# Even and odd token tiles as the two halves, block sums during the attention, and the first feed-forward products in two column parts

## The chip, the cores and the metric

The kernel runs on one core of a Trainium2 chip. The metric is the device time of one execution in microseconds. TensorE (PE) multiplies matrices, VectorE (DVE), ScalarE (ACT) and GpSimd (POOL) do the elementwise work, and SyncE (SP) issues most of the transfers. Each engine works through its own queue in order.

## The reference

Two encoder layers work on 1024 tokens of 1024 channels. In each, a norm and one input projection feed three mixers: a Fourier mix over all tokens, attention in a window (eight query heads, two key groups, blocks of 128 tokens, a learned sink), and attention to 256 memory rows. The three results are normalised apart and go through one output projection. Then comes a gated feed-forward of 2816 channels.

```python
y = jnp.concatenate([_rmsnorm(y_f, ...), _rmsnorm(y_a, ...), _rmsnorm(y_m, ...)], axis=-1) @ w_out[l]
x = x + _rmsnorm(y, g_post_mix[l])
h = _rmsnorm(x, g_pre_ffn[l])
gate, up = jnp.split(h @ w_ffn_in[l], 2, axis=-1)
f = (jax.nn.silu(gate) * up) @ w_ffn_out[l]
x = x + _rmsnorm(f, g_post_ffn[l])
```

## The kernel before

**Arithmetic.** Each operand is split into a high and a low part: ACT casts the high one (line 151), DVE or POOL subtracts it from the source (line 152). One product of two operands is three products on PE: high by high, high by low, low by high. The two feed-forward products are made by Strassen's scheme. The input h is cut into four blocks of 512 channels by 512 tokens (two halves of the channels, two halves of the tokens), and seven products are made of sums of them. `Blocks.tile` turns one token tile of 128 into the four raw blocks: eight transposes `hTp` (line 1033) and two ACT copies (line 1034). `Blocks.sum(i, c)` makes the operand of product i for the columns of one tile (chunk c of four): a sum where the product needs one (line 1051, on POOL for i = 6, else on DVE) and its split. `Blocks.last` (lines 1063 and 1064) makes the differences for products 7 and 3 in place. Weights come in pairs of 128 output columns (`Quad`), a gate quad and an up quad for each of 11 pairs. `weights(i)` makes a sum of weight blocks (line 1094, DVE) and its split, and `product` issues 12 products of 512 columns (line 1104). Products 2 and 4 share the PSUM tile `qy`, 5 and 3 `qz`, 1 and 7 `qx`, and 6 has `qw`.

**Token halves.** Half 0 is tiles 0 to 3, half 1 is tiles 4 to 7, in all stages. Products 2 and 4 need half 0 alone; 5, 1, 6, 7 and 3 need half 1 too.

**The stage around the change.** The window attention runs twice over the eight tiles, once for each key group. The first pass is woven with the other two mixers' output product (`fm_units`). In the second pass, `out_prep(t)` splits both groups' results of tile t (POOL makes the low parts), squares them on ACT, sums the squares with four small products `ssp` (line 925) and takes the root on POOL (line 929). `out(t)` makes the output product `mo` of tile t (24 products), scales it (line 1008, DVE), and goes through the residual norm: square on ACT (line 322), root on POOL (lines 208 and 210), multiply (line 324, DVE), add (line 325, POOL, for the last tile DVE), then the norm ahead of the feed-forward: square (284), root, multiply (289, DVE). After that the tile can be transposed. The loop has eight tiles and a tail of four steps in which the block sums are written; the sums for products 2 and 4 come at steps 8 and 9, the others from step 8 on.

**The order.** The code gives the work in this sequence, and a scheduler with its own costs places each instruction in its engine's queue. Buffers are slots of two arenas by number (`Ring`, `at`), so what may be written when follows from those numbers. The attention's keys, queries and output weights lie in slots that block operands take over later: product 6's operand (slots 32 and 40) lies where the output weights are until the last `mo`.

## Time and profile before

| | |
|---|---|
| median of three runs | 2135.3 us (2132.69 to 2136.14) |
| profiled execution | 2135.5 us, span 2133.7 us |
| mean granted TensorE clock | 0.969 |
| busy: PE, DVE, ACT, POOL | 2013.2, 1577.7, 1060.6, 863.4 us |
| PE busy, 400 to 420 us | 7.29 of 20 us |
| PE busy, 440 to 460 us | 20.00 of 20 us |

A profile row names the line, the engine, what is written and read, the shape and the count. A row of the timeline begins with its start and its duration; a bracket gives the idle time ahead of it and what ended it. A row of the windows gives the stretch and its length, then the busy time of PE, of its weight loads, of DVE, ACT and POOL with the number of instructions, then the granted clock, the share of the transfer engines and GB/s. Rows of the chain of waits give start, duration and what ran. Layer 0 has the way into the feed-forward at about 400 us, layer 1 at about 1450 us.

### The profile page before, as it was taken

What the parts mean: (1) busy time and instruction counts of PE and PEld (TensorE: products, weight loads), DVE (VectorE), ACT (ScalarE), POOL (GpSimd) and SP (SyncE); (2) the same over time, 40 slices, a digit from 0 to 9 for tenths busy, and PEclk for the clock granted to TensorE, in tenths of its full rate; (3) what the DMA queues carried; (4) which work ended last, traced back from release to release, by engine and by line L of the source; (5) the groups of instructions that cost most, each with busy time, mean ns of one, the idle gap of its engine ahead of it and who ended that gap; (6) DMA issues with size and microseconds to landing.
All of it is one profiled execution on the core that took longest, in us unless ns stands there. A gap on an engine that the chain in (4) does not pass through costs nothing.

```text
span 2133.7 us, 28334 instructions
## 1 busy us (share of the span) xinstructions
PE 2013.2 (94%) x9490; PEld 1655.0 (78%) x9490; DVE 1577.7 (74%) x2441; ACT 1060.6 (50%) x2257; POOL 863.4 (40%) x858
## 2 busy tenths in 40 slices
...
GB/s 221 45 50 65 65 94 105 152 65 94 118 101 95 112 94 194 318 221 287 246 138 41 60 64 85 75 137 110 84 129 94 94 111 92 123 249 284 276 261 138
DMA packets 173602, 287.50 MB, mean 135 GB/s; under 512 B 15480, under 2 KB 73360, under 8 KB 173456
## 3 DMA queue, kind: packets, MB, share of 16 engines
...
q8 instruction: 74, 1.21, 0.2%
...
## 4 chain that ended last, share of the span: by engine, by line
PE 74%; DMA 8%; DVE 7%; ACT 4%; POOL 4%; issue 2%; SPq 0%; POOLq 0%; DVEq 0%; ACTq 0%
PE fo L1232 12%; PE qz L1104 11%; PE qx L1104 11%; PE qy L1104 11%; PE mo L162 7%; PE qw L1104 5%; PE kvp L162 4%; PE qp L162 3%; DVE arena_r L152 3%; DMA arena_f<-actd 2%; PE sc L728 2%; PE pT L765 2%; DMA arena_f<-in_w_ffn_out 1%; ACT arena_r L151 1%; PE zT L162 1%
## 5 line engine op out<-in xcount | busy, mean ns | idle before, releaser
L151 ACT CAST arena_r<-arena_f 128x512 fp32r<-128x512 f32 (+1 forms) x780 | 443.1, 591 | 674.0 <-PE qz L1104 115.5
L152 DVE TENSOR_TENSOR arena_r<-arena_f,arena_r 128x512 fp32r<-128x512 f32 (+1 forms) x676 | 536.6, 816 | 182.9 <-ACT arena_r L151 179.6
L1232 PE MATMUL fo<-arena_r 128*128 128x512 f32 x1848 | 432.2, 395 | 17.5 <-ACT arena_r L151 15.1
L1232 PEld LDWEIGHTS fo<-arena_r 128*128 128x128 f32 x1848 | 351.7, 191 | 94.6 <-ACT arena_r L151 17.7
L1104 PE MATMUL qy<-arena_r 128*128 128x512 f32 x1056 | 261.5, 397 | 27.6 <-ACT arena_r L151 16.5
L1104 PEld LDWEIGHTS qy<-arena_r 128*128 128x128 f32 x1056 | 201.5, 192 | 72.0 <-ACT arena_r L151 17.0
L1094 DVE TENSOR_TENSOR arena_f<-arena_f 128x512 f32<-128x512 f32 x220 | 206.0, 939 | 5.1
L1104 PE MATMUL qz<-arena_r 128*128 128x512 f32 x704 | 196.3, 389 | 1.8 <-DVE arena_r L152 1.8
L1124 POOL TENSOR_TENSOR arena_f<-arena_f 128x512 f32<-128x512 f32 x44 | 73.0, 1658 | 292.8 <-ACT arena_f L1109 292.8
L1216 POOL TENSOR_TENSOR arena_f<-arena_f 128x512 f32<-128x512 f32 x50 | 73.6, 1475 | 269.5 <-DVE arena_r L152 136.2
L1104 PEld LDWEIGHTS qz<-arena_r 128*128 128x128 f32 x704 | 132.0, 188 | 29.8 <-DVE arena_r L152 2.4
L1156 POOL TENSOR_TENSOR arena_f<-arena_f 128x512 f32<-128x512 f32 x44 | 73.6, 1674 | 165.6 <-DVE arena_f L1136 119.1
L152 POOL TENSOR_TENSOR arena_r<-arena_f,arena_r 128x256 fp32r<-128x256 f32 (+2 forms) x104 | 88.8, 859 | 118.4 <-ACT arena_r L151 93.3
L1104 PE MATMUL qx<-arena_r 128*128 128x512 f32 x528 | 127.7, 389 | 1.4 <-ACT arena_r L151 1.4
L1104 PE MATMUL qw<-arena_r 128*128 128x512 f32 x528 | 127.6, 389 | 0.0
L1104 PE MATMUL qx<-big,arena_r 128*128 128x512 f32 x528 | 126.8, 389 | 0.0
L1104 PEld LDWEIGHTS qx<-arena_r 128*128 128x128 f32 x528 | 99.1, 188 | 22.5 <-ACT arena_r L151 2.0
L1104 PE MATMUL qz<-big,arena_r 128*128 128x512 f32 x352 | 115.5, 389 | 0.0
L1104 PEld LDWEIGHTS qw<-arena_r 128*128 128x128 f32 x528 | 99.1, 188 | 20.8
L1104 PEld LDWEIGHTS qx<-big,arena_r 128*128 128x128 f32 x528 | 99.1, 188 | 20.6
L162 PE MATMUL mo<-arena_r 128*128 128x512 f32 x384 | 102.6, 406 | 5.5 <-POOL arena_r L152 4.0
L162 PE MATMUL mo<-big,arena_r 128*128 128x512 f32 x384 | 102.3, 404 | 0.0
...
## 6 DMA issues: line engine op xcount, KB each, us to landing
...
actd<-arena_f SPq DMA_DIRECT2D x154, 256.0 KB, 3.7
arena_f<-actd SPq DMA_DIRECT2D x154, 256.0 KB, 4.2
...
```

The source lines that it names most:

```text
L151: nc.scalar.copy(hi, src)
L152: return (lo_eng or nc.vector).tensor_tensor(out=lo, in0=src, in1=f32(hi), op=ALU.subtract)
L162: mm(self.dst, a, b, start=self.i == 0, stop=self.i == self.n - 1)
L728: mm(pt, lhs, self.kst[g][i][:, k0 * P : k1 * P], start=i == 0, stop=i == 1)
L765: nc.tensor.transpose(pT[:, h, :], es_[h // 2][:, h % 2, j * P : j * P + P], ident)
L1094: nc.vector.tensor_tensor(out=s, in0=a, in1=b, op=op)
L1104: mm(pt, a, b, start=start and n == 0, stop=n == 11, skip_group_check=not start)
L1124: nc.gpsimd.tensor_tensor(out=self.v, in0=self.v, in1=self.s2, op=ALU.add)
L1156: (G if i in (0, 3) else V).tensor_tensor(out=a[i], in0=c, in1=g[i], op=ALU.mult)
L1216: (nc.vector, nc.gpsimd)[k % 2].tensor_tensor(out=s, in0=x, in1=y, op=op)
L1232: mm(pt, ab[:, 0, x, sl], ab[:, 1, y], start=new and first and j == 0, stop=last and j == 2, skip_group_check=not new)
```

## The change

Five things are changed. Even tiles are now half 0 and odd tiles half 1, so `divmod(t, 4)` becomes `divmod(t, 2)` with the roles exchanged, and the stages that go through tiles by halves take them in the order 0, 2, 4, 6, 1, 3, 5, 7. The attention keeps the order 0 to 7. A chunk of 128 columns then has all its four raw blocks after two neighbouring tiles.

The loop makes sums of chunks 0 to 2 from step 4 on rather than in the tail. Only chunk 3 needs the last two tiles.

The first group's half of `out_prep` (split, squares, two of four `ssp` products) is made in the first pass by `ya_prep`, and the second pass adds its sum of squares to the stored one.

Products 2 and 4 of the first gate and up quads are made in two column parts, 384 columns as soon as chunks 0 to 2 are there and 128 later (`ahead`). The weight operand is made once and used by both parts.

Buffers move: block operands, weights, raw weights and the sums' slot; the operands of the second feed-forward product have nine slots rather than six in layer 0 (`abs_`, seven for its last product), and the same fifteen in another order in layer 1.

The diff, cut to what is spoken of. Left out are renamed indices, the Fourier stage's sums over tiles (the same six additions), and the tile order in the start and in the last stage:

```diff
@@ -38,7 +38,9 @@
...
 SKEW = 1
-N_SM = {"pos": 1}
+
+TILES = (0, 2, 4, 6, 1, 3, 5, 7)
+N_SM = {"pos": 1, "ssa": 2}
 PS_BUFS = {"sc": 2, "pT": 2, "av": 2, "pd": 2}
...
@@ -125,15 +127,15 @@
...
     ropes = {2: run(6, 4, 0.5), 8: run(36, 6, 2)}
-    ems, es_ring, y1s = run(16, 4, 2), run(33, 5, 3), run(6, 2, 1)
+    ems, es_ring, y0s, y1s = run(16, 4, 2), run(33, 5, 3), run(8, 2, 1), run(6, 2, 1)
     sqs, pms, xfs = run(16, 2, 2), run(20, 2, 2), Ring(16, 20, 24, 28, 32, 0)
-    qws, sns, silus, acts = Ring(32, 0, 16, 20), Ring(36, 38, 40, 42, 32, 34), run(8, 5, 2), run(18, 7, 2)
-    sums, wsums = run(8, 4, 2), Ring(4, 6)
+    qws, sns, silus, acts = Ring(8, 12, 0, 44), Ring(36, 38, 40, 42, 32, 34), run(8, 5, 2), run(18, 7, 2)
+    sums, wsums = Ring(14), Ring(4, 6)
     ras, rbs, bsums, xs_ = run(40, 3, 2), run(46, 6, 2), Ring(58, 32, 34), Ring(36, 24)
...
     zzs, dhs, tabs = run(112, 2, 4), run(64, 2, 4), run(72, 4, 2)
-    mps, phs, yys = run(24, 2, 4), run(16, 3, 4), run(104, 2, 4)
-    wcs, abs_ = Ring(112, 116, 96, 100, 48, 52, 56, 60), Ring(80)
+    mps, phs, yys, y1y = run(24, 2, 4), run(16, 3, 4), run(104, 2, 4), run(104, 4, 2)
+    wcs, abs_ = Ring(24, 28, 112, 116, 120, 48, 52, 56), Ring(80)
...
@@ -291,7 +293,7 @@
...
-        half, c = divmod(t, 4)
+        c, half = divmod(t, 2)
         if c == 0:
...
@@ -789,8 +793,7 @@
...
                 nc.gpsimd.tensor_tensor(out=self.v32[:, 4 * half : 4 * half + 4], in0=f32(v[:, :, 0]), in1=f32(v[:, :, 1]), op=ALU.add)
-            pf = big(4, 2, 2, P, dt=F32)
-            self.pfs, self.pfi = [pf[:, i] for i in range(4)], 0
+            self.pfs, self.pfi = [at(8 + 2 * i, 2, 2, P) for i in range(3)], 0
...
@@ -803,27 +806,23 @@
...
-            self.ya = getattr(self, "ya", {})
             st = {}
...
             def unit(i):
+                if g == 0 and i > SKEW:
+                    self.ya_prep(i - SKEW - 1, st.pop(("y", i - SKEW - 1)))
                 if SKEW <= i < NT + SKEW:
                     n = i - SKEW
-                    half, c = divmod(n, 4)
-                    if g == 0 and n == 0:
-                        ya = at(8, 2, 2, 512)
-                        self.ya[0, 0], self.ya[0, 1] = ya[:, 0], ya[:, 1]
-                    if g == 0:
-                        dst = self.ya[g, half][:, :, c * P : c * P + P]
+                    y = (y1s if g else y0s)(2, P)
+                    self.att_values(g, n, st.pop(n), y)
+                    if g:
+                        self.out_prep(n, y)
                     else:
-                        dst = self.ya[g, n] = y1s(2, P)
-                    self.att_values(g, n, st.pop(n), dst)
-                    if g:
-                        self.out_prep(n)
+                        st["y", n] = y
                 if i < NT:
...
-            return [lambda i=i: unit(i) for i in range(NT + SKEW)]
+            return [lambda i=i: unit(i) for i in range(NT + SKEW + 1 - g)]
...
@@ -923,11 +922,31 @@
...
                 mm(pss, sq[:, i], ones, start=i == 0, stop=i == w - 1)
-            ms = sm(1, "ms")
-            nc.vector.tensor_scalar(out=ms, in0=pss[:, 0:1], scalar1=1.0 / n, scalar2=EPS, op0=ALU.mult, op1=ALU.add)
+            return pss[:, 0:1]
+
+        def rsqrt_pool(self, ms):
             r = sm(1, "grs")
...
             return r
+
+        def group_scale(self, parts, n, ring):
+
+            ms = sm(1, "ms")
+            nc.vector.tensor_scalar(
+                out=ms, in0=self.square_sum(parts, ring), scalar1=1.0 / n, scalar2=EPS, op0=ALU.mult, op1=ALU.add
+            )
+            return self.rsqrt_pool(ms)
+
+        def ya_prep(self, t, y):
+
+            if t == 0:
+                self.yas, self.ssa = {}, sm(NT, "ssa")
+            yy = at((28, 30, 112, 114, 116, 118, 120, 122)[t], 2, 2, P, dt=F32R)
+            split(yy[:, 0], yy[:, 1], y, nc.gpsimd)
+            self.yas[t] = yy
+            nc.vector.tensor_scalar(
+                out=self.ssa[:, t : t + 1], in0=self.square_sum((y,), sqs), scalar1=1.0 / AW, scalar2=EPS, op0=ALU.mult, op1=ALU.add
+            )
...
@@ -983,11 +1002,14 @@
...
-        def out_prep(self, t):
-            half, c = divmod(t, 4)
-            sl = slice(c * P, c * P + P)
-            parts = [self.ya[0, half][:, :, sl], self.ya[1, t]]
-            self.prepped[t] = self.split_y(parts, yys), self.group_scale(parts, AW, sqs)
+        def out_prep(self, t, y):
+            yy = y1y(2, 2, P, dt=F32R)
+            split(yy[:, 0], yy[:, 1], y, nc.gpsimd)
+            ms = sm(1, "ms")
+            nc.vector.scalar_tensor_tensor(
+                out=ms, in0=self.square_sum((y,), sqs), scalar=1.0 / AW, in1=self.ssa[:, t : t + 1], op0=ALU.mult, op1=ALU.add
+            )
+            self.prepped[t] = (self.yas.pop(t), yy), self.rsqrt_pool(ms)
...
@@ -997,14 +1019,14 @@
...
             x, f = self.xf.pop(t)
-            (hi, lo), rs = self.prepped.pop(t)
+            yy, rs = self.prepped.pop(t)
             for n in range(2):
...
                 for i in range(4):
-                    w = self.woa[2 + i]
-                    acc.add(hi[:, i], lo[:, i], w[0][:, ns], w[1][:, ns])
+                    w, y = self.woa[2 + i], yy[i // 2]
+                    acc.add(y[:, 0, i % 2], y[:, 1, i % 2], w[0][:, ns], w[1][:, ns])
                 nc.vector.scalar_tensor_tensor(
...
@@ -1017,13 +1039,13 @@
...
-        HB = {2: (64, 72), 4: (80, 88), 5: (16, 24), 1: (0, 8), 6: (32, 40), 7: (None, None), 3: (None, 104)}
+        HB = {2: (80, 16), 4: (64, 72), 5: (0, 8), 1: (88, 96), 6: (32, 40), 7: (None, None), 3: (None, 104)}
...
         def tile(self, h, t):
-            half, c = divmod(t, 4)
+            c, half = divmod(t, 2)
             for kg in range(2):
...
@@ -1041,19 +1063,13 @@
...
                 self.b[i] = [big(4, 512) if k is None else at(k, 4, 512, dt=F32R) for k in self.HB[i]]
-            if i == 2:
-                s = b11[:, :, sl]
-            if i == 5:
-                s = b22[:, :, sl]
+            hi, lo = (b[:, :, sl] for b in self.b[i])
             if i in (1, 4, 6):
...
                 (nc.gpsimd if i == 6 else nc.vector).tensor_tensor(out=s, in0=x[:, :, sl], in1=y[:, :, sl], op=op)
-            if i == 7:
-                s = b21[:, :, sl]
-            if i == 3:
-                s = b12[:, :, sl]
-            hi, lo = (b[:, :, sl] for b in self.b[i])
+            else:
+                s = self.raw[{2: (0, 0), 5: (1, 1), 7: (0, 1), 3: (1, 0)}[i]][:, :, sl]
             split(hi, lo, s, lo_eng)
...
@@ -1095,13 +1111,15 @@
...
-        def product(self, pt, i, start):
-            w = self.weights(i)
+        def product(self, pt, i, start, sl=slice(0, 512)):
+            if i not in self.ws:
+                self.ws[i] = self.weights(i)
+            w = self.ws[i]
             bh, bl = self.hb.b[i]
...
             for k in range(4):
-                for a, b in ((w[:, 0, k], bh[:, k]), (w[:, 0, k], bl[:, k]), (w[:, 1, k], bh[:, k])):
-                    mm(pt, a, b, start=start and n == 0, stop=n == 11, skip_group_check=not start)
+                for a, b in ((w[:, 0, k], bh[:, k, sl]), (w[:, 0, k], bl[:, k, sl]), (w[:, 1, k], bh[:, k, sl])):
+                    mm(pt[:, sl], a, b, start=start and n == 0, stop=n == 11, skip_group_check=not start)
                     n += 1
...
@@ -1109,14 +1127,21 @@
...
+        def ahead(self, i, sl):
+
+            if i == 2:
+                if sl.start == 0:
+                    self.y = ps([512], "qy", "pT")
+                    self.s2 = sns(512)
+                self.product(self.y, 2, True, sl)
+                nc.scalar.copy(self.s2[:, sl], self.y[:, sl])
+            else:
+                self.product(self.y, 4, False, sl)
+
         def step(self, i):
-            if i == 2:
-                self.y = ps([512], "qy", "pT")
-                self.product(self.y, 2, True)
-                self.s2 = self.snap(self.y)
-            if i == 4:
-                self.product(self.y, 4, False)
+            if i in (2, 4):
+                self.ahead(i, slice(0, 512))
             if i == 5:
...
@@ -1345,26 +1368,30 @@
...
                 mix.out_rows(i - 1, xs[i - 1], pmd[i - 1])
+
+            for n, c in {
+                4: [(2, 0)], 6: [(2, 1), (4, 0), (4, 1)], 7: [(5, 0), (5, 1)], 8: [(2, 2), (4, 2)],
+                9: [(5, 2), (1, 0), (1, 1), (1, 2)], 10: [(2, 3), (4, 3), (6, 0), (6, 1), (6, 2)],
+            }.get(i, ()):
+                hb.sum(n, c)
             if i == NT:
-                for c in range(4):
-                    hb.sum(2, c)
+                sums.ks = (40, 42)
+                gq.load()
+                gq.ahead(2, slice(0, 384))
             if i == NT + 1:
-                gq.load()
-                for c in range(4):
-                    hb.sum(4, c)
-                gq.step(2)
+                uq.load()
+                uq.ahead(2, slice(0, 384))
+                for q in first:
+                    q.ahead(4, slice(0, 384))
             if i == NT + 2:
-                uq.load()
-                gq.step(4)
-                uq.step(2)
-                uq.step(4)
-            if i >= NT:
-                for n in (5, 1):
-                    hb.sum(n, i - NT)
-            if i > NT:
-                for c in (i - NT - 1,) if i < NT + 3 else (2, 3):
-                    hb.sum(6, c)
+                for n in (2, 4):
+                    for q in first:
+                        q.ahead(n, slice(384, 512))
+                for c in range(3):
                     hb.last(c)
+        for n in (5, 1, 6):
+            hb.sum(n, 3)
+        hb.last(3)
         for n in (7, 3):
...
@@ -1403,12 +1431,13 @@
...
             if i == 7:
+                abs_.i, abs_.ks = 0, (80, 88, 96, 104, 112, 48, 56)
                 mix.zf_load()
...
         if not last:
-            norm_T(st.pop(NT - 1), nhT, NT - 1, "av")
+            norm_T(st.pop(NT - 1), nhT, TILES[NT - 1], "av")
...
```

The scheduler's queues show the change best at two places of layer 0. On PE, between the last output product and the first product that needs half 1, before (`mo_3971` and `mo_3985` are tile 7's two column halves of `mo`, `qy_4041` the gate quad's products 2 and 4, `qy_4096` the up quad's):

```order
L162 MATMUL mo_3985<-arena_r 128x512 x4
L1033 MATMUL hTp_4015<-const,arena_f 128x128 x4
L1033 MATMUL hTp_4021<-const,arena_f 128x128 x4
L1104 MATMUL qy_4041<-arena_r 128x512 x2
L1033 MATMUL hTp_4068<-const,arena_f 128x128 x4
L1033 MATMUL hTp_4074<-const,arena_f 128x128 x4
L1104 MATMUL qy_4041<-arena_r 128x512 x22
L1104 MATMUL qy_4096<-arena_r 128x512 x2
L1033 MATMUL hTp_4137<-const,arena_f 128x128 x4
L1033 MATMUL hTp_4143<-const,arena_f 128x128 x4
L1104 MATMUL qy_4096<-arena_r 128x512 x10
L1104 MATMUL qz_4183<-arena_r 128x512
```

And now (`mo_4029` is tile 7's second half, `qy_3998` the gate quad's products, `qy_4084` the up quad's, `hTp_4129` and `hTp_4135` tile 6, `hTp_4211` tile 7):

```order
L164 MATMUL mo_4029<-arena_r 128x512 x12
L1122 MATMUL qy_3998<-arena_r 128x384 x2
L1055 MATMUL hTp_4059<-const,arena_f 128x128 x4
L1055 MATMUL hTp_4065<-const,arena_f 128x128 x4
L1122 MATMUL qy_3998<-arena_r 128x384 x22
L1122 MATMUL qy_4084<-arena_r 128x384 x2
L1055 MATMUL hTp_4129<-const,arena_f 128x128 x4
L1122 MATMUL qy_4084<-arena_r 128x384 x10
L1055 MATMUL hTp_4135<-const,arena_f 128x128 x4
L1122 MATMUL qy_3998<-arena_r 128x128
L1122 MATMUL qy_4084<-arena_r 128x384 x12
L1055 MATMUL hTp_4211<-const,arena_f 128x128 x4
```

Before, 36 products of block operands stood between the last `mo` and the first `qz`, and all transposes of tiles 6 and 7 among them. Now 96 narrower ones stand there, and the first two stand ahead of tile 5's transposes.

On DVE, from the scaling of tile 7's output product on, before:

```order
L1008 SCALAR_TENSOR_TENSOR arena_f<-mo_3985,grs_3896,arena_f 128x512
L1094 TENSOR_TENSOR arena_f<-arena_f 128x512
L152 TENSOR_TENSOR arena_r<-arena_f,arena_r 128x4x128
L152 TENSOR_TENSOR arena_r<-arena_f,arena_r 128x512
L1064 TENSOR_TENSOR big_3942<-big_3942,big_3949 128x4x128
L289 SCALAR_TENSOR_TENSOR arena_f<-arena_f,nrs_3939 128x1024
L152 TENSOR_TENSOR arena_r<-arena_f,arena_r 128x4x128
L324 SCALAR_TENSOR_TENSOR arena_f<-arena_f,rrs_4003 128x1024
```

And now:

```order
L326 SCALAR_TENSOR_TENSOR arena_f<-arena_f,rrs_3965 128x1024
L1009 SCALAR_TENSOR_TENSOR ms_3925<-ssp_3927,ssa_2268 128x1
L1070 TENSOR_TENSOR arena_f<-big_3496,big_3489 128x512
L154 TENSOR_TENSOR arena_r<-big_3489,arena_r 128x4x128
L154 TENSOR_TENSOR arena_r<-arena_f,arena_r 128x4x128
L1030 SCALAR_TENSOR_TENSOR arena_f<-mo_4015,grs_3931,arena_f 128x512
L1030 SCALAR_TENSOR_TENSOR arena_f<-mo_4029,grs_3931,arena_f 128x512
L291 SCALAR_TENSOR_TENSOR arena_f<-arena_f,nrs_3884 128x1024
L291 SCALAR_TENSOR_TENSOR arena_f<-arena_f,nrs_3974 128x1024
L326 SCALAR_TENSOR_TENSOR arena_f<-arena_f,rrs_4047 128x1024
L1110 TENSOR_TENSOR arena_f<-arena_f 128x512
```

The multiply of tile 7's residual norm (`rrs_4003` before, `rrs_4047` now) had five small items and a norm of another tile ahead of it and now has two norms; the first weight sum (line 1094 before, 1110 now) stood ahead of that multiply and now stands behind it.

100 lines of the change are left out of this document (50 added, 50 removed).

## The prediction

> **What bounds the kernel now.** I read the page first, then the windows around the one place where TensorE thins out, then the rows of its queue there.
>
> ```profile
> PE 2013.2 (94%) x9490; PEld 1655.0 (78%) x9490; DVE 1577.7 (74%) x2441; ACT 1060.6 (50%) x2257; POOL 863.4 (40%) x858
> 360.00:380.00 20.00, 19.27 (x114) 13.77 (x112) 13.95 (x30) 12.88 (x36) 14.53 (x18) 1.00 0.42 145
> 380.00:400.00 20.00, 15.47 (x74) 11.62 (x75) 16.89 (x19) 10.94 (x25) 15.63 (x17) 0.92 0.46 136
> 400.00:420.00 20.00, 7.29 (x27) 5.04 (x25) 18.74 (x22) 11.93 (x22) 15.41 (x12) 0.73 0.55 184
> 420.00:440.00 20.00, 16.53 (x66) 12.81 (x67) 17.47 (x25) 12.30 (x24) 6.54 (x3) 0.91 0.09 27
> 440.00:460.00 20.00, 20.00 (x90) 16.56 (x89) 16.89 (x28) 10.07 (x18) 8.32 (x4) 1.00 0.06 14
> 1440.00:1460.00 20.00, 11.57 (x63) 9.02 (x62) 16.77 (x19) 12.05 (x23) 16.45 (x16) 0.88 0.52 166
> 1460.00:1480.00 20.00, 13.38 (x48) 10.08 (x47) 18.27 (x23) 9.32 (x17) 9.48 (x7) 0.70 0.40 132
> ```
>
> TensorE (PE) has work 94% of the span. The windows (length, then PE, weight load, DVE, ACT, POOL, then granted clock, DMA) show the hole that the change aims at: the way from the attention of the second key group into the feed-forward. PE is busy 7.29 of 20 us from 400 to 420, at a clock of 0.73, while DVE is busy 18.74. Layer 1 repeats it at 1440. So outside the hole PE sets the time, inside it DVE and the latency of the last tile do.
>
> ```profile
> 396.41 3.32 PE L162 MATMUL mo<-arena_r 128*128 128x512 f32 x8 [2.78 <-POOL arena_r L152]
> 399.52 1.46 PE L1033 MATMUL hTp<-const,arena_f 128*128 128x128 f32 x8
> 409.06 1.22 PE L1104 MATMUL qy<-arena_r 128*128 128x512 f32 x2 [8.07 <-ACT arena_r L151]
> 412.87 3.11 PE L1104 MATMUL qy<-arena_r 128*128 128x512 f32 x10 [0.43 <-DVE arena_r L152]
> 420.67 5.07 PE L1104 MATMUL qy<-arena_r 128*128 128x512 f32 x14 [4.69 <-ACT arena_f L1109]
> 426.85 0.66 PE L1033 MATMUL hTp<-const,arena_f 128*128 128x128 f32 x4 [0.68 <-ACT big L1034]
> 432.88 2.83 PE L1104 MATMUL qz<-arena_r 128*128 128x512 f32 x11 [1.26 <-DVE arena_r L152]
> 1449.49 1.03 PE L1033 MATMUL hTp<-const,arena_f 128*128 128x128 f32 x8
> 1482.88 2.79 PE L1104 MATMUL qz<-arena_r 128*128 128x512 f32 x11 [0.54 <-DVE arena_r L152]
> ```
>
> The last output product (mo, tile 7) ends at 399.7. From 432.88 on PE has no gap any more. That is 33.2 us, and in layer 1 it is 1482.88 - 1449.5 = 33.4. Call the end of mo(7) zero; everything below is counted from it.
>
> What PE does at full clock comes from merged rows of the chain of waits, each a run without a gap:
>
> ```profile
> 452.02 2.72 PE qx L1104 x12
> 300.34 0.70 PE sc L728 x4
> 894.54 5.75 PE kmp L162 x48
> 881.34 0.87 PE mTp L421 x8
> ```
>
> Per instruction: 0.227 us at 512 columns, 0.175 at 384, 0.120 at 256, and 0.109 for the 128-wide transposes. In the 33.2 us PE did 39 products of 0.227 (2 + 10 + 14 + 10 and three single ones) and 16 transposes, 10.6 us; 22.6 are lost. The first pair of weight blocks has 168 products, so 129 x 0.227 = 29.3 us remain at the solid point: the pair ends at 62.5.
>
> **The change part by part.** *The last tile's chain.* Its rows in layer 0:
>
> ```profile
> 399.82 3.38 DVE L1051 TENSOR_TENSOR arena_f<-big,big 128x512 f32<-128x512 f32 x2
> 405.40 1.40 DVE L1008 SCALAR_TENSOR_TENSOR arena_f<-mo,grs,arena_f 128x512 f32<-128x512 f32 x2
> 406.83 1.06 ACT L322 ACTIVATE arena_f<-arena_f 128x1024 bf16<-128x1024 f32 x1 [0.99 <-DVE arena_f L1008]
> 408.76 0.86 POOL L210 TENSOR_TENSOR rrs<-rrsv,const 128x1 f32<-128x1 f32 x1
> 410.94 1.27 DVE L324 SCALAR_TENSOR_TENSOR arena_f<-arena_f,rrs 128x1024 f32<-128x1024 f32 x1
> 412.74 1.21 DVE L325 TENSOR_TENSOR arena_f<-arena_f 128x1024 f32<-128x1024 f32 x1
> 419.80 1.27 DVE L289 SCALAR_TENSOR_TENSOR arena_f<-arena_f,nrs 128x1024 f32<-128x1024 f32 x1
> ```
>
> DVE comes to tile 7's L1008 only at 405.40, 5.7 us after mo(7), since sums of blocks (L1051) and splits stand ahead of it. In the new order three small items stand between tile 6's residual and tile 7's L1008, so I let it end at 1.1. Then a square (1.3 with its read), two POOL steps (1.5), the multiply (1.2): done at 5.1. In layer 0 the first weight sum (0.6) and its ACT cast (0.6) stand behind that multiply, so PE's first product starts at 6.4 rather than at 9.4: a gap stays. In layer 1 that sum stands ahead of the multiply, the gap is 2.2, but the second quad's weight sum follows seven items later, which by the same steps costs PE some 5 us more: 7.4 in all.
>
> *Column parts.* Blocks 2 and 4 of both quads are 48 products of 512 columns in a layer: 10.9 us. They become 48 of 384 and 48 of 128. The first cost 48 x 0.175 = 8.4. No row shows a 128-wide product of this kind. Below it stands the transpose, 0.109; above it the 512-wide product, 0.227, if a narrow one were no faster. I take 0.120, the 256-wide row: same operand type, and already near what the transpose needs. So 8.4 + 5.8 = 14.2, or 3.3 us a layer more than before; at 0.227 it is 8.4 more, at 0.109 it is 2.7.
>
> The Trainium skill, "TensorE: Matmul & The Clock Gate", section LDWEIGHTS, says that a weight load's time follows its 128 columns (128 / 1.2 = 107 ns), whatever the moving width, which speaks against cutting one product in two: every load is made twice. By it the narrow part would cost 48 x 0.107 = 5.1, not 5.8, so 0.7 us a layer less than my figure, an estimate from that page; the transpose row (0.109) agrees with it.
>
> PE's own sum in the entry: gap 6.4, parts 14.2, 16 transposes 1.7, and 3 for the half clock that the gap leaves behind (as the 0.73 of 400 to 420 does now): 25.3, and 30.4 at the dear price. Then 117 full products (three are single ones ahead) remain.
>
> *DVE.* Here the order decides, since DVE is at 17 to 19 of 20 us. "Sums during the attention" moves less than it says: before, 19 small items of the blocks already stand ahead of tile 7's L1008, now 15 do. From L1008 to the last split that block 6 needs, the new order has 32 small items and 5 of 1024 columns (34 and 4 in layer 1); before, to the split at 432, 25 and 4.
>
> ```profile
> L152 DVE TENSOR_TENSOR arena_r<-arena_f,arena_r 128x512 fp32r<-128x512 f32 x21 | 17.5, 859 | 2.0 <-ACT arena_r L151 1.9
> L1094 DVE TENSOR_TENSOR arena_f<-arena_f 128x512 f32<-128x512 f32 x9 | 6.0, 680 | 0.0
> ```
>
> In 384 to 440 a small item lasts 0.68 to 0.86 by these groups; back to back they overlap by some 0.07, so 0.61 to 0.79. I take 0.69: 32 x 0.69 = 22.1, five wide ones 6.0, 2.2 of waiting for the root of tile 7, and the start at 1.1: 31.4. That is behind PE's own 25.3 and at its dear 30.4. So PE waits for DVE there, and the price of the 128-wide part is mostly hidden by DVE; were DVE faster, it would show in full. The pair ends at 31.4 + 117 x 0.227 = 58.0, against 62.5: 4.5 us a layer, 9 in both. With 0.61 an item it would end at 55.4 and with 0.79 at 61.2.
>
> *Tail of the attention.* The half of the split and the squares that belongs to the first group moves to the pass before. Now PE waits there for POOL:
>
> ```profile
> PE mo L162 <- POOL arena_r L152: 4.0, 3, 2.8
> 213.00:267.00 54.00, 52.04 (x268) 44.65 (x268) 37.97 (x116) 40.85 (x109) 22.25 (x39) 0.91 0.18 64
> 267.00:320.00 53.00, 53.00 (x293) 43.44 (x292) 31.38 (x107) 37.14 (x107) 23.49 (x41) 1.00 0.27 95
> L152 POOL TENSOR_TENSOR arena_r<-arena_f,arena_r 128x256 fp32r<-128x256 f32 x28 | 25.9, 932 | 29.9 <-ACT arena_r L151 13.1 <-PE sc L728 8.4 <-PE ssp L925 4.5
> ```
>
> The 4.0 us go (tile 7's split has one POOL item left, and the block sums on POOL stand behind it). Where it arrives, 8 splits of 0.93 on POOL, as many casts and squares on ACT, lie under a PE that is busy 52 to 53 us of a window, with ACT at 37 to 41. I cost them at nothing; uncovered they would be 7.5 us a layer. The two small products per tile change place only.
>
> *Nothing else.* The halves by even and odd tiles change no instruction count in the start, the Fourier part and the projections. Nine slots for the second product's operands in layer 0 rather than six: nothing taken, at best the 5 us of gaps at 846 and 867, since the DMA queues set that stage.
>
> Sum: 9 + 4 = 13 us from the profiled execution's 2135.5, which stands 0.2 above the median of 2135.3: 2122.5.
>
> **The rivals.**
> *The hole closes.* If DVE items go at 0.61 and the tile's chain is all that is waited for, the pair ends at 55.4 in both layers (14 us), the tail gives 4 and the nine slots 4 of their 5: 2114, or less. For it: PE has 25.3 us of its own in that time. Against it: the 32 items.
> *The narrow product is dear and shows.* At 0.227 PE's own sum ends at 30.4, and if the half clock lasts as long as it does now (some 3 us more), PE, not DVE, sets the pair: 33.4 + 26.6 = 60.0, 2.5 gained in a layer, 5 in both. If the work moved into the pass before is not covered either, its 7.5 us more than take back the tail's 4, and the time is 2130 to 2135. For it: no row shows that a narrow product is fast. Against it: the transposes and the 256-wide rows. This is also the case in which the change doesn't do what it says.
> *DVE becomes slower than now, and the kernel with it.* Small items at 0.94 (the mean of L1094 over the kernel is 939) because POOL's four sums for block 6 now stand in one run beside them: 32 x 0.94 = 30.1 + 6.0 + 2.2 + 1.1 = 39.4, and the pair ends at 66.0, 3.5 later in each layer. With no gain in the tail that is 2142.5. It decides from 0.83 an item on, where the pair ends as late as before. For it: two splits took 3.43 us at 1450.90 beside a POOL add. Against it: the mean in the same stretch now.
>
> ```profile
> L1094 DVE TENSOR_TENSOR arena_f<-arena_f 128x512 f32<-128x512 f32 x220 | 206.0, 939 | 5.1
> 1450.90 3.43 DVE L152 TENSOR_TENSOR arena_r<-arena_f,arena_r 128x512 fp32r<-128x512 f32 x2
> ```
>
> **How the numbers follow.** Forecast 48%, its own range 2116 to 2129; the hole closes 16%; dear and visible 21%; slower DVE 15%. A measurement tells about 0.2% from no change, so 2131.0 to 2139.6 is the same. Faster: the first two, and a fifth of the third, 0.68. Same: most of the third and a few of the last, 0.18. Slower: 0.14. For 8 in 10 the range leaves out the deep end of the second case and the worst of the last: 2108 to 2141.
>
> **What would show it.** The product of 384 columns should first start 5 to 8 us after mo(7) in layer 0; 128-wide products 0.11 to 0.13 apart; PE waiting for DVE splits ahead of blocks 5 and 6; the first pair ending near 58 after mo(7); no wait of mo for POOL. I am wrong if DVE's items ahead of block 6 take under 0.6 or over 0.83 us each, or if the windows before 360 or the second product's stage move by more than 3 us.

## The result and the profile after

The changed kernel takes 2152.6 us (median of four runs, 2151.7 to 2153.7), the kernel before 2134.0 beside it: a ratio of 1.0091, with a 95% interval of 1.0079 to 1.0104. It is slower by 18.6 us where 13 us less were forecast. Its profiled execution has a span of 2149.9 us.

The first line of the page and the windows of the same places as before:

```profile
PE 2021.6 (94%) x9586; PEld 1665.9 (77%) x9586; DVE 1580.2 (74%) x2457; ACT 1061.2 (49%) x2261; POOL 848.8 (39%) x858
380.00:400.00 20.00, 17.37 (x99) 12.44 (x98) 15.38 (x18) 12.79 (x26) 17.62 (x18) 1.00 0.59 192
400.00:420.00 20.00, 11.22 (x50) 9.57 (x49) 18.45 (x21) 9.86 (x19) 9.97 (x11) 0.74 0.61 199
420.00:440.00 20.00, 14.08 (x92) 12.08 (x91) 18.82 (x25) 11.00 (x22) 9.79 (x5) 0.91 0.01 3
440.00:460.00 20.00, 19.82 (x81) 16.25 (x82) 18.82 (x27) 12.02 (x21) 6.02 (x4) 0.91 0.10 27
1480.00:1500.00 20.00, 16.52 (x96) 13.75 (x94) 17.65 (x25) 11.02 (x21) 9.29 (x5) 0.87 0.08 27
```

The hole did not close, it spread: PE is busier from 400 to 420 (11.22 against 7.29) and less busy from 420 to 440 (14.08 against 16.53), and the clock is still 0.91 after 440. DVE is as full as before.

The timeline of PE at that place in layer 0:

```profile
399.99 3.90 PE L164 MATMUL mo<-arena_r 128*128 128x512 f32 x16
412.09 1.01 PE L1122 MATMUL qy<-arena_r 128*128 128x384 f32 x2 [8.21 <-ACT arena_r L153]
432.40 3.15 PE L1122 MATMUL qy<-arena_r 128*128 128x128 f32 x24
437.80 1.22 PE L1122 MATMUL qz<-arena_r 128*128 128x512 f32 x2 [1.96 <-ACT arena_r L153]
440.19 4.74 PE L1122 MATMUL qw<-arena_r 128*128 128x512 f32 x13 [1.17 <-DVE arena_r L154]
```

The last output product ends at 403.9. The first product of 384 columns follows 8.2 us later, and PE is solid from 440.2 on, 36.3 us after that end (33.2 before). The first pair ends at 468.4, 64.5 us after it. Measured the same way, by the last instruction of its PSUM tiles, the kernel before has 63.0.

The loss does not lie in this place alone. The next table is worked out from the starts of single PE instructions in the traces: the first input product (`kvp`) and the first score product (`sc`) of each layer, its last output product (`mo`), a quarter of the way through all `qz` products (layer 0) or three quarters (layer 1), where PE has long been solid, and the first product of the second feed-forward stage (`fo`). Products of the feed-forward between those marks take 206.7 us in all kernels and are left out.

| stage, us | before | after | difference |
|---|---|---|---|
| start to first kvp | 73.2 | 76.3 | +3.2 |
| to first sc (Fourier, projections, memory), layer 0 | 139.7 | 137.7 | -2.0 |
| attention, layer 0 | 186.2 | 189.4 | +3.2 |
| entry, layer 0 | 237.3 | 238.9 | +1.7 |
| second product and transition to layer 1 | 264.0 | 268.8 | +4.8 |
| first kvp to first sc, layer 1 | 164.2 | 162.2 | -2.0 |
| attention, layer 1 | 178.0 | 184.0 | +6.0 |
| entry, layer 1 | 237.1 | 240.9 | +3.8 |
| second product to the end, layer 1 | 240.7 | 238.1 | -2.5 |

The sum is 16.2, the difference of the two spans. Where the forecast had 9 us gained in the entries, 5.5 are lost; where it had 4 gained in the attention, 9.2 are lost; and the start and the way into layer 1, which were to stay, take 3.2 and 4.8 more. Three other rows give 6.5 back.

Each column comes from one profile. Two later runs, before_load_earlier and before_load_later, have the order of the kernel before on every engine up to layer 1's projections. Over these three profiles the start differs by up to 1.4 us, the entry of layer 0 by 2.4, the second product and transition by 2.7, and the attention of layer 0 by 0.1; the last row's stage takes 236.4 to 240.7. So the attention rows are firm, and a single 1.7 or -2.5 in the other rows is not.

### The profile page after: what moved, and what is told of

Read it like the earlier page. It is cut to its first block, busy times and chain, and to the rows that moved or that the text cites. A ratio compares the mean times of both kernels' runs of the same rounds, so it can differ in the third digit from the quotient of the medians.

```text
span 2149.9 us, 28564 instructions
## 1 busy us (share of the span) xinstructions
PE 2021.6 (94%) x9586; PEld 1665.9 (77%) x9586; DVE 1580.2 (74%) x2457; ACT 1061.2 (49%) x2261; POOL 848.8 (39%) x858
## 4 chain that ended last, share of the span: by engine, by line
PE 69%; DMA 9%; DVE 9%; ACT 5%; POOL 4%; issue 4%; SPq 1%; POOLq 0%; DVEq 0%; ACTq 0%
PE qx L1122 11%; PE qz L1122 10%; PE fo L1257 10%; PE qy L1122 10%; PE mo L164 6%; PE qw L1122 5%; PE kvp L164 4%; DMA arena_f<-actd 4%; DVE arena_r L154 3%; PE qp L164 3%; PE sc L732 2%; DMA arena_f<-in_w_ffn_out 2%; PE pT L769 1%; ACT arena_r L153 1%; PE zT L164 1%
## 5 line engine op out<-in xcount | busy, mean ns | idle before, releaser
L1122 PE MATMUL qy<-arena_r 128*128 128x512 f32 (+2 forms) x1152 | 266.4, 380 | 22.0 <-ACT arena_r L153 17.6
L1122 PEld LDWEIGHTS qy<-arena_r 128*128 128x128 f32 x1152 | 210.9, 191 | 63.5 <-ACT arena_r L153 19.7
L1110 DVE TENSOR_TENSOR arena_f<-arena_f 128x512 f32<-128x512 f32 x220 | 212.0, 967 | 12.2 <-DMA arena_f<-in_w_ffn_in 4.6
L1149 POOL TENSOR_TENSOR arena_f<-arena_f 128x512 f32<-128x512 f32 x44 | 66.3, 1507 | 311.9 <-ACT arena_f L1127 311.9
L1241 POOL TENSOR_TENSOR arena_f<-arena_f 128x512 f32<-128x512 f32 x50 | 71.1, 1422 | 277.6 <-DVE arena_r L154 190.1
L1181 POOL TENSOR_TENSOR arena_f<-arena_f 128x512 f32<-128x512 f32 x44 | 73.4, 1668 | 175.7 <-DVE arena_f L1161 128.7
L154 POOL TENSOR_TENSOR arena_r<-arena_f,arena_r 128x256 fp32r<-128x256 f32 (+2 forms) x104 | 84.3, 815 | 124.0 <-ACT arena_r L153 106.1
```

Source lines behind the costliest of these rows:

```text
L154: return (lo_eng or nc.vector).tensor_tensor(out=lo, in0=src, in1=f32(hi), op=ALU.subtract)
L1110: nc.vector.tensor_tensor(out=s, in0=a, in1=b, op=op)
L1122: mm(pt[:, sl], a, b, start=start and n == 0, stop=n == 11, skip_group_check=not start)
L1149: nc.gpsimd.tensor_tensor(out=self.v, in0=self.v, in1=self.s2, op=ALU.add)
L1181: (G if i in (0, 3) else V).tensor_tensor(out=a[i], in0=c, in1=g[i], op=ALU.mult)
L1241: (nc.vector, nc.gpsimd)[k % 2].tensor_tensor(out=s, in0=x, in1=y, op=op)
```

## The experiments

Each run was timed beside the kernel before on one chip; ratios are to that kernel.

### The start

```diff
-            split(hT[half][0][kg][...], hT[half][1][kg][...], pt)
+            latest["split"] = split(hT[half][0][kg][...], hT[half][1][kg][...], pt)
...
-                    TT(A[:, i], V[i, 0], V[i, 1], ALU.add)
-                    TT(B[:, i], V[i, 0], V[i, 1], ALU.subtract)
+                    with tc.issue_after(latest["split"].ins):
+                        TT(A[:, i], V[i, 0], V[i, 1], ALU.add)
+                        TT(B[:, i], V[i, 0], V[i, 1], ALU.subtract)
```

> The changed kernel with one thing altered: the two Fourier additions that need only the even tiles stand in DVE's queue behind the last split of the normed input, as all four did in the kernel before; nothing is left out. In the changed kernel the first input product (kvp) starts at 76.3 us, in the kernel before at 73.2. Theory 1 (the new place of these two additions, 1.22 us each, is what holds up the last splits and so the first product of the Fourier part): kvp starts at 73.2 again, within 0.5, and the whole is about 3 us shorter than the changed kernel's 2152.6, so 2149 to 2150. Theory 2, the prediction's step (the new halves cost nothing in the start, so the 3.2 us have another cause): kvp stays at 76 and the time at 2152 to 2153.

Timelines of DVE and PE in the changed kernel:

```profile
59.95 1.22 DVE L521 TENSOR_TENSOR arena_f<-arena_f 128x1024 f32<-128x1024 f32 x1
...
62.28 1.22 DVE L521 TENSOR_TENSOR arena_f<-arena_f 128x1024 f32<-128x1024 f32 x1
64.15 12.35 PE L164 MATMUL zT<-arena_r 128*128 128x512 f32 x46 [1.54 <-DVE arena_r L154]
```

The same two timelines in this run:

```profile
61.81 1.30 DVE L154 TENSOR_TENSOR arena_r<-hTp,arena_r 128x512 fp32r<-128x512 f32 x2 [0.16 <-ACT arena_r L153]
63.03 2.35 DVE L523 TENSOR_TENSOR arena_f<-arena_f 128x1024 f32<-128x1024 f32 x2
73.13 2.20 PE L164 MATMUL kvp<-big,arena_r 128*128 128x512 f32 x9
```

With even tiles as half 0, two of the six additions need half 0 only. The scheduler puts them ahead of the last splits, and PE waits 1.54 us and then runs at a lower clock (0.72 granted from 64 to 70 us; 46 products in 12.35 us, where 48 take 11.46 in this run). Queued behind, kvp starts at 73.1: theory 1. But the whole got slower, 2161.1 us (1.0145, 1.0117 to 1.0172): from that place on the scheduler made another order, with 192.3 and 190.9 us of attention. Theory 1 holds for the stage, not for the total.

### POOL beside DVE

In the changed kernel's entry, timelines of DVE and POOL:

```profile
401.13 2.79 POOL L327 TENSOR_TENSOR arena_f<-arena_f 128x1024 f32<-128x1024 f32 x1
401.59 2.88 DVE L154 TENSOR_TENSOR arena_r<-big,arena_r 128x512 fp32r<-128x512 f32 x1
421.38 3.41 POOL L1070 TENSOR_TENSOR arena_f<-big,big 128x512 f32<-128x512 f32 x1 [3.70 <-DVE arena_r L154]
430.19 4.65 DVE L154 TENSOR_TENSOR arena_r<-arena_f,arena_r 128x512 fp32r<-128x512 f32 x4
431.04 3.25 POOL L1070 TENSOR_TENSOR arena_f<-big,big 128x512 f32<-128x512 f32 x2 [3.13 <-DVE arena_r L154]
```

A split of 0.68 us takes 2.88 and ends just after POOL's addition beside it; four that take 2.5 take 4.65. At 421.38 it is POOL that is held up, 3.41 us for an addition that takes 1.3 elsewhere. The Trainium skill, "SBUF — State Buffer", section "Who interferes with whom", says that a DVE instruction with two SBUF inputs contends with a GpSimd instruction that reads SBUF, and that the pair of ports they share is an exclusive lock; these rows agree with it. The chain of waits of this place, in order of time, shows it as "issue" between pieces of one instruction, and runs on DVE for the most part:

```profile
401.66 0.75 DVE arena_r L154
402.42 1.98 issue
...
430.26 0.75 DVE arena_r L154 x2
431.02 0.37 issue
431.39 1.94 DVE arena_r L154 x2
433.33 1.43 issue
```

The first run takes POOL's additions away; it is the changed kernel otherwise:

```diff
-                (nc.gpsimd if i == 6 else nc.vector).tensor_tensor(out=s, ...)
+                nc.vector.tensor_tensor(out=s, ...)
...
-            nc.gpsimd.tensor_tensor(out=b21, in0=b21, in1=b22, op=ALU.add)
+            nc.vector.tensor_tensor(out=b21, in0=b21, in1=b22, op=ALU.add)
...
-            residual(x, f, self.gpost, nc.gpsimd if t < NT - 1 else nc.vector)
+            residual(x, f, self.gpost, nc.gpsimd if t < NT - 2 else nc.vector)
```

> The changed kernel with POOL's three kinds of wide work in the way into the feed-forward given to DVE: the four sums for product 6, the four additions of the differences for products 7 and 3, and the residual addition of tile 6; nothing is left out. Theory 1 (an addition on DVE and one on POOL do not run side by side: in the changed kernel five groups of DVE's items between 401 and 436 us are 1.1 to 2.2 us longer than the same items alone, 7.7 us in all, each beside a POOL item that ends with it): the 5.4 to 6 us that DVE gets in addition are less than what it no longer waits, so the first pair ends 2 to 5 us earlier in each layer and the time is 2143 to 2149. Theory 2 (the number of DVE's items is what sets the pair, POOL's work is free): 9 more items, 5.5 to 6 us later in each layer, 2160 to 2165.

The group of DVE's splits from the last output product to the solid point (403.9 to 440.7 us) in the changed kernel; the columns are busy time, mean ns of one, and idle time ahead:

```profile
L154 DVE TENSOR_TENSOR arena_r<-arena_f,arena_r 128x512 fp32r<-128x512 f32 x17 | 15.4, 936 | 0.0
```

The same group in this run (405.2 to 437.6 us):

```profile
L154 DVE TENSOR_TENSOR arena_r<-arena_f,arena_r 128x512 fp32r<-128x512 f32 x15 | 10.2, 684 | 0.0
```

The timeline of PE in this run:

```profile
402.96 2.11 PE L164 MATMUL mo<-arena_r 128*128 128x512 f32 x8 [0.75 <-POOL arena_r L154]
409.95 1.01 PE L1122 MATMUL qy<-arena_r 128*128 128x384 f32 x2 [4.88 <-ACT arena_r L153]
435.99 1.19 PE L1122 MATMUL qz<-arena_r 128*128 128x512 f32 x4 [1.07 <-DVE arena_r L154]
```

One split falls from 936 to 684 ns, PE is solid 30.9 us after the last output product, and the pair ends at 57.6 and 56.3 us: the 58.0 that were forecast. The time is 2142.9 us (1.0054, 1.0037 to 1.0070), 9.7 less than the changed kernel's by the two medians and some 8 by the two ratios. Theory 1, and more than it said (6.9 and 9.9 us less entry, 2 to 5 expected); what follows the hole runs at full clock too (1.00 granted from 440 to 460 us, 0.91 in the changed kernel). Part of the gain is hidden: layer 1's attention, in another order, takes 188.8 us for 184.0.

The same three edits in the kernel before:

> The kernel before, with POOL's wide work in the way into the feed-forward given to DVE as in the run tail_on_dve (the four sums for product 6, the four additions for products 7 and 3, the residual addition of tile 6). Nothing is left out. In the kernel before, DVE's items in that stretch are 5.5 us (layer 0) and 6.1 us (layer 1) longer than the same items alone, and 4.8 us of work come to DVE in each layer. Theory 1 (what an addition on POOL costs DVE beside it bounds the way into the feed-forward in both kernels, so the change's own entry is no shorter without it): the first pair ends 3 to 6 us earlier in each layer, time 2121 to 2128. Theory 2 (it is the change's run of four sums that collides, the kernel before suffers little): the pair ends within 1.5 us of where it did, time 2131 to 2137.

2129.7 us (0.9997, 0.9986 to 1.0008). Attention and entry together are 6.1 us shorter in layer 0 (417.4; 5.7 of it in the attention) and 3.0 longer in layer 1 (418.1, its attention at 184.2). Neither theory as a whole: the first fits layer 0, and in layer 1 another order of the attention stands in the way. Its entry alone, 236.9 and 233.9 us, is longer than the 232.0 and 231.0 of the changed kernel with the same edits. So the change does shorten the entry, by 4.9 and 2.9 us, where POOL is out of the way; the second figure is little more than the 2.4 us by which profiles of one order differ.

Two more runs leave out one of the edits, chosen since TensorE's order in layer 1's attention then stays as before. The first has the sums and the differences on DVE, the second the differences and the residual:

> The kernel before with the four sums for product 6 and the four additions for products 7 and 3 on DVE in both layers, tile 6's residual addition left on POOL; nothing is left out. Unlike in before_tail_on_dve the scheduler keeps the order of TensorE in the attention of layer 1 (98.7% of it the same as before). Theory 1 (the additions on POOL hold DVE up in the way into the feed-forward of the kernel before too, and what the other run lost in layer 1 came of its order): attention of layer 1 within 2 us of 178.0, attention and entry together 3 to 6 us shorter in each layer, time 2121 to 2127. Theory 2 (in the kernel before the additions on POOL cost nothing that counts): 423.5 and 415.1 us within 2, time 2129 to 2134.

> The kernel before with the four additions for products 7 and 3 and tile 6's residual addition on DVE in both layers, the four sums for product 6 left on POOL; nothing is left out. TensorE's order in the attention of both layers is the same as before. Theory 1 (each kind of addition on POOL holds DVE up by more than its own 0.60 us on DVE): attention and entry together 2 to 4 us shorter in each layer, since four additions of 1.3 us and one of 2.7 us on POOL become 0.6 and 1.2 us on DVE; time 2124 to 2129. Theory 2: within 2 us, time 2129 to 2134.

The first takes 2128.7 us (0.9982, 0.9970 to 0.9995): 4.9 us less in layer 0's attention and entry, none in layer 1's (415.6). Its profile is that of the slowest of twelve executions (2138.1 us), so these stages say little. The second takes 2121.2 us (0.9946, 0.9934 to 0.9958), 10.5 us less than the kernel before, and is the fastest of all kernels here: 416.3 and 412.8 us for 423.5 and 415.1. TensorE's order in the attention is that of the kernel before in both layers. Theory 1 there, by more than the 2 to 4 us expected in layer 0 and at the lower end in layer 1.

The changed kernel with the second set of edits:

> The changed kernel with the four additions for products 7 and 3 and tile 6's residual addition on DVE, as in the run before_tail_no_sums; the four sums for product 6 stay on POOL, nothing is left out. It tells what the change is worth where POOL holds DVE up less: before_tail_no_sums took 2121.2 us, with 235.0 and 235.8 us from the last output product to the quarter mark of the seventh products in layers 0 and 1. Theory 1 (freed of POOL, the change's entry is the shorter one, and what it loses lies in the attention and the start): 231 to 235 us in both layers, attention 187 to 192 us, time 2140 to 2148. Theory 2 (the change's entry is no shorter in any case): 236 to 240 us, time 2147 to 2155.

2152.2 us (1.0090, 1.0070 to 1.0110), no gain on the total; its executions lie far apart (2143.2 to 2156.7), and the profile is that of the slowest. The entries, 235.4 and 234.4 us, are 3.5 and 6.5 us shorter than the changed kernel's, but no shorter than the 235.0 and 235.8 of the kernel before with the same edits. The attention, 191.3 and 192.3, takes the gain back. Theory 2 on the time; the entries lie at the upper end of theory 1. As long as the sums for product 6 stand on POOL, the change's entry is no better than the old one with the same edits.

### The column parts

```diff
-                gq.ahead(2, slice(0, 384))
+                gq.ws[2] = gq.weights(2)
...
-                        q.ahead(n, slice(384, 512))
+                        q.ahead(n, slice(0, 512))
```

> The changed kernel with products 2 and 4 of the first quads made in one piece of 512 columns again, after all four chunks; their weight operands are made at the same places as in the changed kernel, nothing is left out. The two column parts cost PE 5.1 us in all (1937.7 against 1932.6 us of products at full clock). Theory 1, the prediction's step (DVE sets the end of the first pair, PE's price is hidden): the pair's end moves by less than 1 us in each layer, or up to 2 us later since the first product starts later than 8.2 us after the last output product; time 2152 to 2156. Theory 2 (the price shows): 2.6 us less in each layer, time about 2147.

2150.9 us (1.0094, 1.0070 to 1.0118), on the total not to be told from the changed kernel's. The entry is 3.1 and 5.3 us shorter (235.9 and 235.6), so the price shows, and more than the price: theory 2 on the place. (The 3.1 alone would be near the 2.4 us by which profiles of one order differ.) Layer 1's attention, with the same work in another order, takes 191.7 us for 184.0 and hides it.

### The sums during the attention

```diff
-                4: [(2, 0)], 6: [(2, 1), (4, 0), (4, 1)], 7: [(5, 0), (5, 1)], 8: [(2, 2), (4, 2)],
-                9: [(5, 2), (1, 0), (1, 1), (1, 2)], 10: [(2, 3), (4, 3), (6, 0), (6, 1), (6, 2)],
+                8: [(2, 0), (2, 1), (2, 2), (5, 0), (1, 0)], 9: [(4, 0), (4, 1), (4, 2), (5, 1), (1, 1), (6, 0)],
+                10: [(2, 3), (4, 3), (5, 2), (1, 2), (6, 1), (6, 2)],
```

> The changed kernel with the sums of blocks for chunks 0 to 2 written in the tail again (steps 8 to 10 of the loop), column parts, halves and moved squares as in the changed kernel; nothing is left out. About ten small items of DVE, 0.60 us apart back to back, come back behind tile 7's scaling. Theory 1, the prediction's step (DVE's items from there on set the first pair): the pair ends 4 to 6 us later after the last output product than the changed kernel's 64.5, and the attention is at most 4 us shorter; time 2152 to 2160. Theory 2 (what the early sums spare in the tail they cost in the attention, where DVE and ACT hold up PE): the sum of attention and entry is the same within 2 us in each layer or shorter, time 2146 to 2154.

2152.3 us (1.0098, 1.0084 to 1.0112): the same. Attention and entry together take 427.6 and 425.2 us (428.4 and 424.9 with the early sums). Theory 2 on the sums of the stages, but its reason fits one layer only. In layer 0 the late sums make the attention 2.2 us shorter and the entry 1.4 longer; in layer 1 the attention is 7.7 us longer (191.7) and the entry 7.4 shorter (233.5), the other way round. Nor do the late sums simply come behind tile 7's scaling, as was expected: in layer 0 that scaling now ends 10.4 us after the last output product rather than 2.5, with more of DVE's items ahead of it.

### The first group's work in the first pass

The move alone, in the kernel before:

> The kernel before with one part of the change alone: the first key group's split, squares and two of four small products are made in the first pass; halves, sums, products and all other buffers as before. Theory 1, the prediction's step: the tail loses the 4.0 us in which the output product waits for POOL, and the moved work lies under other work, so the last output product of layer 0 ends about 4 us earlier (at 395 to 397, it was 399.1) and the time is about 2130. Theory 2 (the moved casts and squares stand in ACT's queue ahead of or among the exponentials of the first pass, whose results PE waits for; in the changed kernel the attention of layer 0 takes 1.2 us longer and that of layer 1 6.1 us longer): no gain in layer 0, 2 to 6 us lost in layer 1, time 2135 to 2141.

2139.4 us (1.0040, 1.0022 to 1.0058). Attention 184.9 and 187.7 us for 186.2 and 178.0: theory 2, with 9.7 us lost in layer 1 where it had 2 to 6. The next two runs move one half each. The splits alone, the squares alone:

> The kernel before, with only the split of the first key group's results moved into the first pass (a cast on ACT and a subtraction of 0.73 us on POOL for each tile); their squares and all four small products stay in the second pass. Nothing is left out. From a layer's first score product to the last product of the other mixers' output the kernel before takes 89.8 and 87.0 us (layers 0 and 1), and with split and squares moved 95.0 and 97.9. Theory 1 (the split on POOL and ACT holds the first pass up): 93 to 98 us in both layers, and the wait for POOL in the second pass is gone; time 2133 to 2140. Theory 2 (the squares do): 88 to 91 us in both, the second pass 2 to 4 us shorter in layer 0; time 2127 to 2131. Theory 3 (the moved work is covered, and what differs is the order that the scheduler makes): the two layers go apart, one within 2 us of the kernel before and one 5 or more above it.

> The kernel before, with only the squares of the first key group's results and their two small products moved into the first pass (0.42 us on ACT and 0.2 to 0.4 us on PE for each tile); the splits stay in the second pass. Nothing is left out. Theory 1 (the split is what costs): 89 to 92 us from the first score product to the last product of the other mixers' output in both layers (89.8 and 87.0 before), time 2130 to 2135. Theory 2 (the squares, in ACT's queue among the exponentials, are what costs): 93 to 98 us in both, time 2135 to 2142. Theory 3 (order): the two layers go apart, by more than 4 us against the kernel before.

The timeline of PE with the first score and the last output products of layer 1, in the kernel before:

```profile
1271.27 0.50 PE L728 MATMUL sc<-arena_r 128*128 128x256 f32 x2 [0.46 <-ACT arena_f L846]
1448.13 1.52 PE L162 MATMUL mo<-arena_r 128*128 128x512 f32 x6
```

The same in the run with the splits moved:

```profile
1266.88 0.50 PE L729 MATMUL sc<-arena_r 128*128 128x256 f32 x2 [0.46 <-ACT arena_f L845]
1445.71 1.77 PE L163 MATMUL mo<-arena_r 128*128 128x512 f32 x7
```

The same in the run with the squares moved:

```profile
1267.06 0.63 PE L729 MATMUL sc<-arena_r 128*128 128x256 f32 x2
1452.20 1.54 PE L163 MATMUL mo<-arena_r 128*128 128x512 f32 x6
```

With the splits moved, the first pass (to the last product of the other mixers) takes 86.9 and 85.7 us (89.8 and 87.0 before), the attention 183.0 and 180.2; 2134.3 us (1.0005, 0.9996 to 1.0014). With the squares moved, 92.5 and 97.9, attention 183.5 and 186.3; 2135.8 us (1.0016, 1.0003 to 1.0030). Over the whole attention both moves gain in layer 0 (3.2 and 2.7 us) and lose in layer 1 (2.2 and 8.3). In the first pass the splits are covered in both layers: theory 2 in the main, though the time is not as low as it said. The squares are as dear there as their theory 2 said, but the layers also go apart (2.7 and 10.9 us more), which was theory 3, the order; three controls further down bear on it. (Some of the longer first pass is only work that now lies in it.)

Why the squares cost, two runs on top of before_square_first were to tell: the squares on DVE, and their small products in the scores' pair of PSUM buffers.

```diff
-                nc.scalar.activation(sq[:, 2 * i : 2 * i + 2], p_, AF.Square)
+                nc.vector.tensor_tensor(out=sq[:, 2 * i : 2 * i + 2], in0=p_, in1=p_, op=ALU.mult)
```

> The run before_square_first with one thing altered: the moved squares of the first key group are made on DVE (one multiplication of 128 x 256 for each tile) and no longer on ACT; nothing is left out. In before_square_first the attention of layer 1 takes 186.3 us (178.0 in the kernel before), that of layer 0 183.5 (186.2). Theory 1 (the squares stand in ACT's queue among the exponentials and the copies that TensorE waits for): layer 1 comes down to 177 to 181, layer 0 stays at 182 to 184, time 2125 to 2131. Theory 2 (it is not ACT but what follows the squares, the small products and their PSUM buffer, or the order): layer 1 stays at 184 to 190, time 2133 to 2138.

```diff
-            pss = ps([2], "ssp", "av")
+            pss = ps([2], "ssp", "sc")
```

> The run before_square_first with one thing altered: the two small products of the moved squares get their PSUM tile from the pair of buffers that the scores use and no longer from the pair that the products with the values use; nothing is left out. Theory 1 (the eight additional tiles in the values' pair hold the values' products up): attention of layer 1 down from 186.3 to 177 to 181 us, layer 0 at 180 to 184, time 2125 to 2131. Theory 2 (ACT, as in the run before_square_on_dve): layer 1 stays at 184 us or more, time 2133 to 2140, since the scores now wait for the same tiles.

On DVE, layer 1's attention is 183.5 us, between the two theories, layer 0's 186.2, and the time 2138.1 us (1.0034, 1.0023 to 1.0045). In the other pair: 199.5 and 202.5 us of attention, 2173.1 us (1.0194, 1.0177 to 1.0211). Theory 1 falls in both. ACT is a part of it at most (2.8 of the 8.3 us in layer 1, with layer 0 2.7 us longer), and whose buffers such small tiles take can cost 37 us. What makes the squares dear is not settled.

### The order alone

Three controls change only where the loads of the output weights are written in layer 1 (one tile earlier, one later; the third one tile earlier, with the squares moved as in before_square_first), which makes the scheduler place the same work otherwise:

```diff
-        weave(mix.att_units(0), fm[:6] + [mix.out_load] + fm[6:])
+        weave(mix.att_units(0), fm[: 6 - l] + [mix.out_load] + fm[6 - l :])
```

> A control: the kernel before with the loads of the attention's output weights written one tile earlier in the first pass of layer 1, so that the scheduler puts the same work of that pass in another order; everything up to there has the same order, and nothing is left out. From the first score product of layer 1 to the last output product the kernel before takes 178.0 us, and the three kernels run so far whose first pass differs take 184.0 to 191. Theory 1 (the squares and splits that were moved into the first pass cost this): 177 to 180 us, time 2131 to 2136. Theory 2 (the order of layer 1 in the kernel before is a fortunate one, and any other order of the same work loses): 183 to 190 us, time 2138 to 2145.

> A second control of the order: the kernel before with the loads of the attention's output weights written one tile later in the first pass of layer 1 (before_load_earlier had them one tile earlier: attention 180.0 us where the kernel before has 178.0). Everything up to there has the same order, nothing is left out. Theory 1 (without the moved squares any order of this pass stays near the old time): 176 to 182 us, time 2129 to 2135. Theory 2 (the order alone is worth as much as the moved squares): 183 us or more, time 2136 to 2141.

> The same control for the moved squares: the run before_square_first (attention of layer 1: 186.3 us) with the loads of the output weights written one tile earlier in the first pass of layer 1; nothing is left out. Theory 1 (the moved squares are what costs, in whatever order): 183 to 190 us, time 2133 to 2140. Theory 2 (before_square_first only met a bad order): 176 to 182 us, time 2127 to 2131.

Without the moved squares, layer 1's attention takes 178.0, 180.0 and 181.6 us in three orders; with them 186.3 and 185.7. The times are 2135.1 (1.0021, 1.0010 to 1.0031), 2136.6 (1.0021, 1.0009 to 1.0032) and 2133.4 us (1.0004, 0.9993 to 1.0015). In the attention theory 1 holds in all three (the second one's time lies where theory 2 had it), though the stages are not sharp: in the third the first score product stands earlier in the program's order. Counted from kvp to the last output product, the three orders without the moved squares take 342.2, 343.1 and 345.6 us and the two with them 349.1 and 346.4, so the cost of the squares in layer 1 lies between 1 and 7 us by this count. On the totals the order weighs as much as the squares.

### The slots of the second product

```diff
-        abs_.ks = (80, 16, 64, ...) if last else (80, 64, 72, 88, 96, 104, 48, 56, 112)
+        abs_.ks = (64, 72, 80, ...) if last else (80, 88, 48, 56, 96, 104)
...
-                abs_.i, abs_.ks = 0, (80, 88, 96, 104, 112, 48, 56)
```

> The changed kernel with the slots of the second product's operands as in the kernel before: six in layer 0, none exchanged for its last product, and the old order in layer 1; all else as changed, nothing is left out. Theory 1, the prediction's step (nothing comes of the nine slots): from the first second-layer product of the feed-forward (849.2 us) to the first input product of layer 1 and from there to the end nothing moves by more than 2 us, time 2151 to 2155. Theory 2 (the nine slots let loads run ahead of those that are needed first): the two gaps of 4.2 and 3.7 us at 852 and 875 become those of the kernel before (3.4 and 1.7), 2 to 3 us less in layer 0, and layer 1 loses the 3.0 us that it has gained; time 2150 to 2154, with the two stages moved in opposite directions.

Second product and transition take 270.6 us in layer 0 (268.8 with nine slots) and 235.5 in layer 1 (238.1): theory 1 in layer 0, and in layer 1 a gain of 2.6 where theory 2 had a loss (the stage takes 236.4 to 240.7 without any edit to it, so this says little). Yet the time is 2159.6 us (1.0135, 1.0118 to 1.0153). The 8.6 us more in layer 1's attention (192.6) are order: PE's sequence there agrees to 99.5% with that of full_width, which took 191.7, and to 54% with that of the changed kernel, which took 184.0. In layer 0 the sequence is the changed kernel's, and the time too (188.7 and 189.4).

### Both repairs

The run tail_on_dve with the moved squares on DVE:

> The run tail_on_dve (changed kernel, all of POOL's wide work in the entry on DVE: 2142.9 us) with the first group's moved squares on DVE in place of ACT; nothing is left out. Attention there: 189.3 and 188.8 us in layers 0 and 1. Theory 1 (the moved squares on ACT are what costs in the first pass): attention 182 to 186 us in both layers, time 2130 to 2137. Theory 2 (not ACT: small products, buffers or the order): 187 us or more in at least one layer, time 2139 to 2147.

2134.4 us (1.0011, 1.0001 to 1.0022): the changed kernel, with POOL's wide work and the moved squares on DVE, is as fast as the kernel before. Entries 232.0 and 230.0 us; attention 185.6 in layer 0 (theory 1), 188.6 in layer 1 (theory 2). The two profiles differ by 3.5 us where the medians of this run and tail_on_dve differ by 8.5, so the stages account for part of the gain only, and the order of the attention is another one too. The kernel before with its best repair, before_tail_no_sums, stays some 13 us ahead.

## Why the prediction was wrong, by its own steps

The forecast was 13 us less, and the two profiled spans differ by 16.2 us the other way. Of these 29 us, 14.5 are the entries, 13.2 the attention, and 8.0 the start and the way into layer 1; the other stages give 6.5 back. The first step that failed is the price of DVE's items in the entry, the second is the cost of nothing for the work moved into the first pass.

**DVE's items: the count was right, the price was not.** From tile 7's scaling to the split that block 6 needs there were 32 small items in layer 0, as counted. But the scaling ended 2.5 us after the last output product, not 1.1 (the 2.88 us split stands ahead of it), and the items lasted 25.0 / 32 = 0.78 us each, not 0.69 (406.4 to 440.1, less 6.0 for the wide ones and 2.7 of waits). That makes 36.3 rather than 31.4: 2.9 us from the items, 1.4 from the late scaling and 0.5 from waits, one of them (1.18 us) for a sum on POOL. The lower clock that the spread gaps leave adds 1.6 (the first 13 products from 440.2 on take 0.36 us each, not 0.227): 64.5 for 58.0. The step that failed is the mean of "0.61 to 0.79", with the start at 1.1 beside it. The 0.78 lies inside that range and inside the bounds that the prediction set for being wrong, but it is the dear end, and with the other two terms it passes the 61.2 named for that end. The low end of the range is about the item alone, the high end a mean of items alone and beside POOL; the prediction took the middle, and the new order puts POOL's sums beside DVE's. The third rival said so, priced it at 0.94 and gave it 15%. With POOL's additions gone, an item takes 0.60 and the pair ends at 57.6 and 56.3. So the 58.0 describes the kernel without POOL's additions.

**PE's price.** Its size was right: 24 products of 128 columns in 2.71 us in the run tail_on_dve, 0.113 each, against 0.120 taken. That DVE hides it was wrong: in one piece the entry is 3.1 and 5.3 us shorter. The Trainium skill's figure for a weight load ("TensorE: Matmul & The Clock Gate", section LDWEIGHTS), 107 ns, lies as near to the 0.113 on the other side.

**The attention's tail.** The wait for POOL did not go. PE's waits in layer 0's attention in the changed kernel (total, times, longest):

```profile
PE mo L164 <- ACT arena_f L987: 2.8, 2, 2.2
PE mo L164 <- ACT arena_r L153: 1.6, 1, 1.6
PE mo L164 <- POOL arena_r L154: 1.2, 1, 1.2
```

PE's waits in layer 1's attention:

```profile
PE mo L164 <- POOL arena_r L154: 2.1, 1, 2.1
PE ssp L924 <- ACT arena_f L921: 2.0, 2, 1.8
```

The 4.0 us were found in layer 0 only, and there the moved splits do gain 3.2. "I cost them at nothing" nearly holds for the splits (2.2 us lost in layer 1) and fails for the squares in layer 1 (8.3 us, or 1 to 7 counted from kvp). The price kept for the case without cover, 7.5 us a layer, comes near that 8.3 by chance: it was the price of eight splits on POOL, and the squares are not on POOL. Cover was read from the shares of busy time, with ACT at 37 to 41 of 53; that ACT's queue is where the squares hold PE up is not shown, and it stays open why layer 1 loses where layer 0 gains.

**"The halves change no instruction count."** Even so the start is 3.2 us dearer: what changed is when two additions become ready. Of the 4.8 us in the second product and the transition, no run shows the cause. Six slots do not take them away, and neither does the place of the two additions. All eight forms of the changed kernel take 268.8 to 273.0 us there, eleven of the twelve forms of the old one 260.4 to 266.0 and one 269.4. They stay open. Both moves are over the 3 us that the prediction named as a sign of being wrong.

**The slots at nothing** was right, as far as profiles that differ by some 3 us can tell.

**The whole.** Every part of the change, undone or taken alone, moves some stage by 2 to 8 us, and several totals hide it, since the scheduler then orders layer 1's attention anew: 184 to 193 us over all forms of the changed kernel. A forecast of 13 us from stage sums did not allow for that.
